# Both seams of a two-layer diffusion block redone, and later landings in the planner that orders it

## The chip, the cores and the metric

The kernel runs on one core of one Trainium2 chip. Its time is the device time of one execution in microseconds. The kernel before takes 2654.45 us, the median of three runs (2653.88 to 2655.54).

## The reference

A backbone of two layers works on 512 latent tokens and 256 context tokens, 1024 wide, all in float32. Cut to what matters here:

```
for l in range(2):
    zx = modulate(rms_norm(x, g_norm1[l]), ...) @ w_in[l]      # and zc from the context tokens
    k, q, v, gates = parts of zx;  kc, vc = parts of zc        # K and V are the first thing formed
    yc = windowed_attention(rope(q), rope(k), v, kc, vc, sink[l])
    ya = bidirectional RG-LRU;  yb = spatial gating MLP
    x = x + ga1 * ((ga*(ya@wb0) + gb*(yb@wb1) + gc*(yc@wb2)) @ w_out[l])
    x = x + ga2 * relu2(modulate(rms_norm(x, g_norm2[l]), ...) @ w_ff1[l]) @ w_ff2[l]
    # the context tokens go the same way in layer 0 and are dropped after layer 1's K, V and scan states
```

There are two kinds of seam in it. An RMS norm needs all of x, so the first matrix product after a norm waits for the residual sum before it: once where the MLP of layer 0 ends and K and V of layer 1 begin, and once in each layer where the output projection ends and the MLP begins.

## The kernel before

Activations lie with channels on the partitions and tokens along the row: 768 columns in layer 0 (512 latent, 256 context), 512 in layer 1. Each product is taken in three parts: a weight block of 128x1024 comes from DRAM as `wr`, ScalarE rounds it to `wh`, VectorE forms the rest `wl` = wr - wh, activations are split in the same way, and TensorE adds wh.h, wh.l and wl.h in PSUM (`fm`, line 866; 24 matmuls a block, 128 output channels and a token range). There are three buffers each of wr, wh and wl (line 49), and 48 slots for activations.

The order of the instructions is not that of the code. All operations are recorded first, and `schedule` (line 337) plans them on the five engines with a cost for each: an operation may be taken up to `WINDOW` = 275 operations ahead of the oldest one not yet done (line 407), if a buffer is free, and the one of the highest priority that is ready in the plan's own time goes first. For a DMA the plan takes bytes/360 ns on one shared line and 1900 ns for the landing (lines 471 and 472), whatever engine issues it. Each engine then works through its list in that order on the chip, and waits where the plan was wrong.

Around the seams the MLP is written as eight chunks (`ff`, line 1401): chunk c of the first product (4 blocks, relu and square) one ahead of chunk c of the second (4 blocks, each giving two output ranges, added to x at once). So that a norm has something to lie beside, some blocks are done by token streams (`streams`, line 811: 0 to 512 and 512 to 768 in layer 0, 0 to 256 and 256 to 512 in layer 1): first stream 1 of these blocks, then the norm of stream 1, then stream 2 of the same blocks, whose weights are loaded and split again. By streams go: the last six of the eight blocks of the output projection (`JOINT` = 2 are done whole, line 525), the first chunk of the MLP, and in layer 0 the last chunk of its second product.

Of layer 1, 44 weight blocks are split already during the MLP of layer 0 and stored in DRAM as pairs (`store`, line 587; `hd` and `ld` in the rows), when VectorE and ScalarE have room. `weights` (line 574) fetches a stored pair into a wh and a wl buffer. The four blocks 112 to 115 are those of K and V of layer 1 (`B_K`), used by `kv_proj` (line 945) right behind the seam, once for the latent and once for the context tokens. `kv_post` (line 951) then forms the constants of the layer, `layer_consts` (line 742: rope tables, sink, the softplus of the LRU, some forty small VectorE instructions, one Exp on ScalarE and three DMAs of GpSimd).

`mod_dve` (line 713) forms one column of the modulation vectors: a wr buffer with rows of w_mod, times the condition, summed (the `junk<-wr,condb` rows). These run beside the merges of the branches.

Of the kernel before, what the change touches and what calls it, by code (L numbers as in the profile page):

```python
# [19 lines left out]
F32R = mybir.dt.float32r  # L20
BF16 = mybir.dt.bfloat16
I32 = mybir.dt.int32
AF = mybir.ActivationFunctionType
# [5 lines left out]
DEPTH = 2  # L29
# [28 lines left out]
LAZY = 200  # L58
DRAINS = 50
FULL, URGENT = 6, 150  # L60
WINDOW = 275
TABLES = {"Sigmoid": (2,), "Sqrt": (3,), "Gelu_apprx_tanh": (11,), "Exp": (0,), "Tanh": (0, 2, 11)}

# [119 lines left out]
class Rec:  # L183
# [153 lines left out]
    def schedule(self):  # L337
# [90 lines left out]
        while events:  # L428
            now = events[0][0]
            while events and events[0][0] <= now + 1e-6:  # L430
                _, _, kind, x = heapq.heappop(events)
                if kind == "rel":
                    used[x.tag] -= 1
                    places[x.tag].append(x)
                    live[x.tag][x.first:x.last + 1] -= 1
                    if x.early:
                        early[x.tag][x.early[0]:x.early[1]] -= 1
            for e in range(5):
                while free[e] <= now + 1e-6:
                    best = pick(e)  # L440
                    if best is None:
                        break
                    _, j, i = best
                    cand[e].pop(j)
                    op = ops[i]
                    for b in op.new:
                        if b.space == "dram":
                            continue
                        used[b.tag] += 1
                        b.early = None  # L450
                        b.prev = places[b.tag].pop(0)
                        if b.prev is None:
                            b.place = fresh[b.tag]
                            fresh[b.tag] += 1
                        else:
                            b.place = b.prev.place
                        if b.first > front:
                            b.early = (front, b.first)
                            early[b.tag][front:b.first] += 1
                    dur = op.dur  # L460
                    if op.both and free[POOL] > now and busy:
                        dur += free[POOL] - now
                    if e == POOL:
                        busy = not op.nbytes
                    if e == ACT and op.table and table not in op.table:
                        dur += 1283
                        table = op.table[0]
                    free[e] = now + dur
                    end = now + dur
                    if op.nbytes:  # L470
                        dma = max(dma, end) + op.nbytes / 360.0
                        end = dma + 1900
                    op.end = end
                    for b in op.psum:
                        b.acc[e] = end
                    order.append((now, i))
                    done[i] = True
                    push(free[e], "go", None)
                    for u in op.users:
                        q = ops[u]  # L480
                        r = end + (LAT if op.nbytes else LATS[e][q.eng])
                        q.ready = max(q.ready, r)
                        q.wait -= 1
                        if q.wait == 0:
                            bisect.insort(cand[q.eng], (q.prio, u))
                            push(q.ready, "go", None)
                    for b in op.bases:
                        b.left -= 1
                        b.end = max(getattr(b, "end", 0.0), end)
                        if b.left == 0 and b.space != "dram":  # L490
                            push(b.end + LAT, "rel", b)
                    while done[front]:
                        front += 1
# [28 lines left out]
AHEAD_C = ('', '0', '1', '2', 'k', '')  # L522
AHEAD_X = ('', '0', '1', 'k')
NEAR = 60
JOINT = (2,)
EARLY = [*range(B_K, B_F2), *range(B_G, B_P), *range(B_AX, B_V)]


# [1 line left out]
class Net:  # L530
# [43 lines left out]
    def weights(self, l, blk):  # L574
        rec = self.rec
        rec.boost, was = self.wboost, rec.boost
        if (l, blk) in self.stored:
            hi = self.wtile("wh", [128, 1024], F32R)
            lo = self.wtile("wl", [128, 1024], F32R)
            for t, d in zip((hi, lo), self.stored[l, blk]):  # L580
                rec.sync.dma_start(t.bitcast(F32), d.bitcast(F32))
        else:
            hi, lo = self.parted(l, blk)
        rec.boost = was
        return hi, lo
# [365 lines left out]
    def kv_post(self, l, ps, pairs):  # L951
        nc = self.nc
        if pairs[0] == 0:
            self.layer_consts(l)
            self.kr, self.VS = [], []
        n = 8 * len(pairs)
        ss = self.tiny(n, "kss")
        h3 = lambda u: u.rearrange("p (a d) -> p a d", d=64)
        for c, i in enumerate(pairs):
            q = self.slot([128, 512])  # L960
            for t in range(2):
                nc.scalar.activation(q[:, t * 256:t * 256 + 256], ps[2 * i + t][:, 0:256], AF.Square)
            nc.vector.tensor_reduce(ss[:, c * 8:c * 8 + 8], h3(q), axis=AX.X, op=OP.add)
        rs = self.head_rs(ss, n, 1.0, "k")
        for c, i in enumerate(pairs):
            u = self.slot([128, 512])
            for t in range(2):
                nc.vector.tensor_mul(h3(u[:, t * 256:t * 256 + 256]), h3(ps[2 * i + t][:, 0:256]),
                                     rs[:, c * 8 + t * 4:c * 8 + t * 4 + 4, None].to_broadcast([128, 4, 64]))
            o = self.slot([128, 512])  # L970
            if i < 2:
                self.rope_rows(u, 2, 2 * i, o)
            else:
                self.gain_rows(u, 2, o)
            self.kr.append(o)
        for t in range(2 * pairs[0], 2 * pairs[-1] + 2):
            v = self.slot([128, 4, 128], F32R)
            s = ps[t][:, 256:512].rearrange("p (g d) -> p g d", d=64)
            nc.scalar.activation(v[:, :, 0:64], s, AF.Copy)
            nc.vector.tensor_sub(v[:, :, 64:128], s, v[:, :, 0:64].bitcast(F32))  # L980
            self.VS.append(v)
# [419 lines left out]
    def ff(self, l, hs, W):  # L1401
        nc = self.nc

        def ff1(c, parts):
            out = [(self.slot([128, W], F32R), self.slot([128, W], F32R)) for _ in range(4)]
            for z in parts:
                for j in range(4):
                    w = self.weights(l, B_F1 + 4 * c + j)
                    if len(parts) == 1:
                        self.ahead()  # L1410
                    ps = self.fm(w, hs, z)
                    for p, a, b in ps:
                        r = self.slot([128, b - a])
                        nc.scalar.activation(r, p, AF.Relu)
                        nc.vector.tensor_mul(r, r, r)
                        self.split(r, out[j][0][:, a:b], out[j][1][:, a:b])
            return out

        def ff2(c, z, parts):
            for j in range(4):  # L1420
                w = self.weights(l, B_F2 + 4 * c + j)
                if c < 7:
                    self.ahead()
                for i in range(2):
                    ps = self.fm(w, z, parts, kk=4, off=i * 128, stride=256)
                    self.residual(l, 40, ps, 2 * j + i)

        z = ff1(0, [[q] for q in self.streams(W)])
        self.aside = False
        for c in range(7):  # L1430
            for _ in range(3):
                self.bg()
            z2 = ff1(c + 1, [self.parts(W)])
            ff2(c, z, self.parts(W))
            z = z2
        if l == DEPTH - 1:
            ff2(7, z, self.parts(W))
            return
        self.mod_bias(l + 1, 0, 16)
        hs = self.pairs(TOK)  # L1440
        G = self.gain(l + 1, 0, TOK)
        ps = [self.p1() for _ in range(6)]
        for q in self.streams(W):
            ff2(7, z, [q])
            self.norm(l + 1, 0, hs, G, *q)
        for toks in (range(4), range(4, 6)):
            self.kv_proj(l + 1, hs, ps, toks)
            self.kv_post(l + 1, ps, (0, 1) if toks[0] == 0 else (2,))
        return hs, ps

    def run(self):
# [149 lines left out]
```

## Time and profile before

| | |
|---|---|
| median of the runs | 2654.45 us |
| the profiled execution | 2655.47 us |
| its span, first to last instruction | 2653.7 us |
| TensorE busy | 2604.5 us (98%) |
| VectorE busy | 1840.1 us (69%) |
| ScalarE busy | 1200.1 us (45%) |
| granted TensorE clock, mean | 0.995 |

The span is what the instructions cover; the profiled execution's own time is 1.8 us more. TensorE is the engine with almost no idle time, so a change shows in the total where it takes a wait of TensorE away, adds one, or changes how long matmuls run. All recorded operations carry the line of the helper that emits them (L508), so rows are told apart by tiles: p is a PSUM tile, s an activation slot, wh and wl the parts of a weight block, t a small tile.

### The profile page before, as it was taken

The numbers are of one execution on the slowest core, as the hardware profiler recorded it, in microseconds if no ns is written. First come the engines' busy times: TensorE is split into PE (matmuls) and PEld (weight loads), VectorE is DVE, ScalarE is ACT, GpSimd is POOL, SyncE is SP. The second block draws the span as 40 slices with busy tenths as digits, with TensorE's granted clock in tenths as the row PEclk, the third lists the DMA queues.
The fourth block names the chain that finished last, engine by engine and source line by source line (L and its number), as shares of the span: only waits on it lengthen the run. The fifth ranks groups of instructions, "written<-read, shape, count | busy, mean of one in ns | idle before, by whom it ended". The sixth has DMA issues, their size and how long they took to land.

```text
span 2653.7 us, 38578 instructions
## 1 busy us (share of the span) xinstructions
PE 2604.5 (98%) x14916; PEld 2246.2 (85%) x14916; DVE 1840.1 (69%) x3504; ACT 1200.1 (45%) x1987; POOL 122.7 (5%) x217
## 2 busy tenths in 40 slices
PE   7999999999999999999999989999999999999999
PEld 4989988888898888888888878888887888888887
DVE  8888776997637748465666678886986567844444
ACT  4566557993122225332333334667993233532322
POOL 1000000011000000100111000000011000000000
PEclk9999999999999999999999999999999999999999
DMA  6122213466425424766778634334577565533332
GB/s 248 45 69 74 61 56 104 122 198 226 154 80 165 162 79 134 230 214 199 246 261 263 207 134 169 105 121 154 159 245 248 165 189 178 158 95 96 95 93 83
DMA packets 129528, 403.54 MB, mean 152 GB/s; under 512 B 15232, under 2 KB 25632, under 8 KB 129344
## 3 DMA queue, kind: packets, MB, share of 16 engines
q1 hardware_dynamic: 99360, 302.11, 36.3%
q0 software_dynamic: 23072, 83.24, 9.4%
q10 hardware_dynamic: 6912, 15.73, 1.6%
q8 instruction: 117, 1.92, 0.3%
q14 instruction: 67, 0.55, 0.1%
HBM read 319.23 MB, written 81.79 MB: 151 GB/s over the span
## 4 chain that ended last, share of the span: by engine, by line
PE 69%; DVE 6%; ACT 3%; issue 1%; DMA 1%; ACTq 0%; DVEq 0%; POOLq 0%
PE p L508 69%; DVE s L508 4%; ACT s L508 3%; DVE wl L508 1%; DMA wr<-wmod 1%; DVE t L508 1%; ACT L508 0%; ACT wh L508 0%; DMA ya<-s 0%; DVE junk L508 0%; ACTq L508 0%; DVEq L508 0%; POOLq L508 0%
## 5 line engine op out<-in xcount | busy, mean ns | idle before, releaser
L508 PE MATMUL p<-s,wh 128*128 128x512 f32 (+1 forms) x6816 | 1670.7, 353 | 8.8 <-DVE s L508 6.1
L508 PEld LDWEIGHTS p<-s,wh 128*128 128x128 f32 x6816 | 1192.0, 189 | 239.7 <-DVE s L508 7.8
L508 PE MATMUL p<-s,wl 128*128 128x512 f32 (+1 forms) x3408 | 1028.5, 351 | 8.8 <-DVE wl L508 8.8
L508 ACT ACTIVATE wh<-wr 128x1024 fp32r<-128x1024 f32 x336 | 354.8, 1059 | 871.7 <-PE p L508 475.0
L508 PEld LDWEIGHTS p<-s,wl 128*128 128x128 f32 x3408 | 570.3, 189 | 58.2 <-DVE wl L508 11.1
L508 DVE TENSOR_TENSOR wl<-wr,wh 128x1024 fp32r<-128x1024 f32 x336 | 409.7, 1222 | 291.8 <-ACT wh L508 249.6
L508 ACT ACTIVATE s<-p 128x512 f32<-128x512 f32 (+6 forms) x598 | 282.0, 511 | 271.1 <-PE p L508 255.2
L508 PE MATMUL p<-wh,s 128*128 128x256 f32 (+1 forms) x1472 | 301.9, 298 | 1.7 <-DVE s L508 1.0
L508 DVE TENSOR_TENSOR s<-s,s 128x512 fp32r<-128x512 f32 (+5 forms) x361 | 258.1, 728 | 53.4 <-ACT s L508 49.0
L508 PE MATMUL p<-s,s 128*128 128x256 f32 (+3 forms) x1568 | 279.9, 319 | 5.9 <-ACT s L508 3.9
L508 ACT ACTIVATE s<-s 128x512 fp32r<-128x512 f32 (+6 forms) x301 | 182.5, 633 | 195.7 <-DVE s L508 179.3
L508 PEld LDWEIGHTS p<-s,s 128*128 128x128 f32 (+1 forms) x1568 | 219.5, 183 | 41.0 <-DVE s L508 7.3
L508 PEld LDWEIGHTS p<-wh,s 128*128 128x128 f32 x1472 | 236.3, 188 | 13.7 <-DVE s L508 2.3
L508 DVE SCALAR_TENSOR_TENSOR s<-p,mod,s 128x512 f32<-128x512 f32 (+1 forms) x222 | 138.7, 646 | 156.2 <-PE p L508 155.5
L508 PE MATMUL p<-wl,s 128*128 128x256 f32 (+1 forms) x736 | 217.9, 296 | 1.0 <-DVE wl L508 1.0
L508 DVE SCALAR_TENSOR_TENSOR junk<-wr,condb 128x1024 bf16<-128x1024 f32 x128 | 156.4, 1222 | 86.7 <-DMA wr<-wmod 85.7
L508 DVE TENSOR_TENSOR s<-p,s 128x512 fp32r<-128x512 f32 (+4 forms) x324 | 182.8, 595 | 37.3 <-ACT s L508 31.5
L508 PEld LDWEIGHTS p<-wl,s 128*128 128x128 f32 x736 | 138.5, 188 | 6.6 <-DVE wl L508 1.6
L508 ACT ACTIVATE s<-s,t,t 128x512 f32<-128x512 f32 (+1 forms) x128 | 109.9, 863 | 50.2 <-DVE t L508 49.8
L508 DVE SCALAR_TENSOR_TENSOR s<-s,s 128x768 f32<-128x768 f32 x128 | 116.7, 949 | 16.2 <-ACT s L508 16.2
L508 PE MATMUL p<-ident,s 128*128 128x128 f32 (+1 forms) x776 | 102.9, 274 | 5.2 <-DVE s L508 3.1
L508 PEld LDWEIGHTS p<-ident,s 128*128 128x128 f32 (+1 forms) x776 | 88.4, 142 | 14.1 <-ACT s L508 3.5
(90 smaller groups left out, 1236.2 us busy)
## 6 DMA issues: line engine op xcount, KB each, us to landing
wr<-w SPq DMA_DIRECT2D x336, 512.0 KB, 3.8
wr<-wmod SPq DMA_DIRECT2D x80, 512.0 KB, 4.2
wl<-ld SPq DMA_DIRECT2D x48, 512.0 KB, 4.8
wh<-hd SPq DMA_DIRECT2D x48, 512.0 KB, 3.7
hd<-wh POOLq DMA_DIRECT2D x44, 512.0 KB, 3.7
ld<-wl POOLq DMA_DIRECT2D x44, 512.0 KB, 5.6
gd<-s ACTq DMA_DIRECT2D x24, 384.0 KB, 2.6
s<-gd POOLq DMA_DIRECT2D x24, 384.0 KB, 5.7
```

Source lines behind the costliest of these rows:

```text
L508: ins = getattr(getattr(self.nc, name), method)(*[r(x) for x in a], **{q: r(x) for q, x in k.items()})
```

## The change

Six things. The planner takes 2600 ns for the landing of a DMA of SyncE or ScalarE and 4800 ns for one of GpSimd, in place of 1900 ns for all. Fetches of the stored K blocks may be planned at most `CLOSE` = 160 operations ahead in place of 275. The constants of layer 1 are formed in the MLP of layer 0, after its fourth round and at a low priority, not behind the seam. Two of the four blocks of chunk 6 of the second product in layer 0 move behind chunk 7 of the first product and are done by streams, together with those of chunk 7. In layer 1 two of the four blocks of chunk 1 of the first product are done by streams, together with those of chunk 0. One block of the output projection is done whole in place of two.

```diff
+LANDS = {SP: 2600, ACT: 2600, POOL: 4800}
@@ schedule
                         dma = max(dma, end) + op.nbytes / 360.0
-                        end = dma + 1900
+                        end = dma + LANDS[e]
@@
+CLOSE = 160
+CONSTS = 4
+SPLIT = 2
+OVER = (0, 1)
+THIRDS = ((0, 512), (512, 768))
-JOINT = (2,)
+JOINT = (1,)
@@ weights
+            rec.far = CLOSE if B_K <= blk < B_Q else None
             for t, d in zip((hi, lo), self.stored[l, blk]):
                 rec.sync.dma_start(t.bitcast(F32), d.bitcast(F32))
+            rec.far = None
@@ kv_post
         if pairs[0] == 0:
-            self.layer_consts(l)
+            if l == 0:
+                self.layer_consts(l)
@@ ff
-        def ff1(c, parts):
-            out = [(self.slot([128, W], F32R), self.slot([128, W], F32R)) for _ in range(4)]
-            for z in parts:
-                for j in range(4):
+        def room():
+            return [(self.slot([128, W], F32R), self.slot([128, W], F32R)) for _ in range(4)]
+        def ff1(c, parts, out, js=range(4)):
+            for j in js:
...
-        z = ff1(0, [[q] for q in self.streams(W)])
+        z, z1 = room(), room() if l == DEPTH - 1 else None
+        for q in self.streams(W):
+            ff1(0, [q], z)
+            if z1:
+                ff1(1, [q], z1, OVER)
         for c in range(7):
...
-            z2 = ff1(c + 1, [self.parts(W)])
-            ff2(c, z, self.parts(W))
+            if c == CONSTS and l < DEPTH - 1:
+                rec = self.rec
+                rec.boost, was = -LAZY, rec.boost
+                self.layer_consts(l + 1)
+                rec.boost = was
+            if c == 0 and z1:
+                z2 = ff1(1, self.parts(W), z1, [j for j in range(4) if j not in OVER])
+            else:
+                z2 = ff1(c + 1, self.parts(W), room())
+            ff2(c, z, self.parts(W), range(4) if c < 6 or l == DEPTH - 1 else range(SPLIT))
...
-        for q in self.streams(W):
+        for q in THIRDS:
+            ff2(6, z6, [q], range(SPLIT, 4))
             ff2(7, z, [q])
             self.norm(l + 1, 0, hs, G, *q)
```

In SyncE's list before the seam between the layers, before the change, the lo part of block 112 and of block 113 stand ahead of the last five raw blocks of the MLP:

```order
L508 DMA wr_14765<-w 128x1024
L508 DMA wl_14789<-ld_112_10941 128x1024
L508 DMA wh_14793<-hd_112_10919 128x1024
L508 DMA wr_14821<-w 128x1024
L508 DMA wl_14877<-ld_113_11019 128x1024
L508 DMA wr_14949<-w 128x1024
L508 DMA wr_14988<-w 128x1024
L508 DMA wr_15028<-w 128x1024
L508 DMA wr_15068<-w 128x1024
L508 DMA wr_15110<-w 128x1024
L508 DMA wh_15225<-hd_113_11000 128x1024
```

At the same place after the change, up to the hi part of block 113:

```order
L509 DMA wr_14919<-w 128x1024
L509 DMA wr_14958<-w 128x1024
L509 DMA wr_14998<-w 128x1024
L509 DMA wr_15038<-w 128x1024
L509 DMA wl_15066<-ld_112_10960 128x1024
L509 DMA wr_15113<-w 128x1024
L509 DMA wl_15206<-ld_113_11038 128x1024
L509 DMA wh_15248<-hd_112_10944 128x1024
L509 DMA wh_15300<-hd_113_11028 128x1024
```

One raw block follows the first fetch of a lo part, where six did, and none follows the second, where five did.

On TensorE, behind the second norm's broadcast (`ones`) in the MLP of layer 1, before the change; the rows ahead of it are the last of stream 1, those behind it the first two blocks of stream 2:

```order
L508 MATMUL p_22805<-s_22679,wh_22710 128x256
L508 MATMUL p_22805<-s_22609,wl_22725 128x256
L508 MATMUL p_22849<-s_22839,ones 128x256
L508 MATMUL p_22885<-s_22528,wh_22749 128x256
L508 MATMUL p_22885<-s_22592,wh_22749 128x256
L508 MATMUL p_22885<-s_22528,wl_22770 128x256
L508 MATMUL p_22890<-s_22528,wh_22809 128x256
```

After the change; p_22895 is the fifth block of stream 1:

```order
L509 MATMUL p_22895<-s_22551,wh_22801 128x256
L509 MATMUL p_22895<-s_22612,wh_22801 128x256
L509 MATMUL p_22895<-s_22551,wl_22815 128x256
L509 MATMUL p_22906<-s_22886,ones 128x256
L509 MATMUL p_22895<-s_22573,wh_22801 128x256
L509 MATMUL p_22895<-s_22635,wh_22801 128x256
L509 MATMUL p_22895<-s_22573,wl_22815 128x256
```

Six of the fifth block's 24 matmuls stand ahead of the broadcast; 18 of it and 24 of the sixth stand between the broadcast and the first of stream 2.

On VectorE, where the merge of the last branch begins in layer 1, before the change; `s<-s,s` of 512 are the lo parts of its eight inputs, junk is a column of the modulation:

```order
L508 TENSOR_TENSOR s_20482<-s_19995,s_20255 128x512
L508 TENSOR_TENSOR s_20489<-s_20026,s_20480 128x512
L508 TENSOR_TENSOR s_20498<-s_20063,s_20487 128x512
L508 SCALAR_TENSOR_TENSOR junk,mod_10721<-wr_20467,condb 128x1024
L508 TENSOR_TENSOR wl_20521<-wr_20462,wh_20493 128x1024
L508 TENSOR_TENSOR s_20537<-s_20086,s_20507 128x512
L508 SCALAR_TENSOR_TENSOR s_20363<-s_20363,p_20472 128x512
L508 TENSOR_TENSOR s_20551<-s_20096,s_20515 128x512
L508 TENSOR_TENSOR s_20556<-s_20113,s_20519 128x512
```

After the change:

```order
L509 TENSOR_TENSOR s_20530<-s_20075,s_20505 128x512
L509 TENSOR_TENSOR wl_20539<-wr_20479,wh_20516 128x1024
L509 TENSOR_TENSOR s_20548<-s_20102,s_20512 128x512
L509 SCALAR_TENSOR_TENSOR s_20385<-s_20385,p_20487 128x512
L509 TENSOR_TENSOR s_20560<-s_20109,s_20532 128x512
L509 TENSOR_TENSOR s_20567<-s_20131,s_20541 128x512
L509 TENSOR_TENSOR s_20572<-s_20207,s_20543 128x512
L509 TENSOR_TENSOR s_20577<-s_20497,s_20565 128x512
L509 SCALAR_TENSOR_TENSOR junk,mod_10735<-wr_20500,condb 128x1024
```

The column of the modulation stands behind the lo parts of all eight inputs, where it stood behind three of them.

## Rows read from the trace of the kernel before

**Rows 1.** The page: the span, and busy time of each engine.

```profile
span 2653.7 us, 38578 instructions
PE 2604.5 (98%) x14916; PEld 2246.2 (85%) x14916; DVE 1840.1 (69%) x3504; ACT 1200.1 (45%) x1987; POOL 122.7 (5%) x217
```

**Rows 2.** Waits of TensorE, whole span: us in total, times, longest.

```profile
PE p L508 <- DVE s L508: 22.5, 17, 6.6
PE p L508 <- DVE wl L508: 9.8, 9, 2.5
PE p L508 <- ACT s L508: 8.3, 10, 1.7
```

**Rows 3.** Waits of TensorE at the seam between the layers, 1515 to 1566 us.

```profile
PE p L508 <- DVE wl L508: 8.8, 7, 2.5
PE p L508 <- DVE s L508: 1.0, 1, 1.0
```

**Rows 4.** Waits of TensorE at layer 1's norm, 2290 to 2306 us.

```profile
PE p L508 <- DVE s L508: 3.4, 2, 2.2
PE p L508 <- ACT s L508: 1.7, 1, 1.7
```

**Rows 5.** Waits of TensorE where layer 1's last merge begins, 2036 to 2046 us.

```profile
PE p L508 <- DVE s L508: 3.3, 1, 3.3
PE p L508 <- ACT s L508: 0.5, 1, 0.5
```

**Rows 6.** Stretches: length, busy us of PE, PEld, DVE, ACT, POOL, clock, DMA.

```profile
1030.00:1515.00 485.00, 485.00 (x2795) 424.92 (x2794) 290.85 (x444) 162.91 (x234) 48.51 (x91) 1.00 0.70 229
1552.30:1555.80 3.50, 3.23 (x13) 2.71 (x13) 2.21 (x8) 0.59 (x2) 0.00 (x0) 0.51 0.00 0
2043.80:2050.70 6.90, 5.22 (x12) 4.05 (x13) 5.86 (x9) 0.14 (x1) 1.08 (x2) 0.51 0.94 338
2299.80:2306.70 6.90, 5.07 (x23) 5.07 (x24) 5.22 (x14) 1.98 (x5) 0.00 (x0) 0.51 0.19 69
```

**Rows 7.** Timeline of SyncE and VectorE at the seam: start, us, what.

```profile
1500.87 0.33 SPq L508 DMA_DIRECT2D wl<-ld  x1
1509.27 0.32 SPq L508 DMA_DIRECT2D wl<-ld  x1
...
1549.04 0.16 DVE L508 TENSOR_SCALAR t<-p 128x4 f32<-128x4 f32 x1 [0.75 <-PE p L508]
...
1551.29 1.22 DVE L508 TENSOR_TENSOR wl<-wr,wh 128x1024 fp32r<-128x1024 f32 x1
```

**Rows 8.** Timeline of TensorE, layer 1: matmuls of 512 and of 256 columns.

```profile
2030.31 0.40 PE L508 MATMUL p<-s,wl 128*128 128x512 f32 x1
...
2040.07 0.40 PE L508 MATMUL p<-s,wl 128*128 128x512 f32 x1
...
2280.12 0.28 PE L508 MATMUL p<-s,wl 128*128 128x256 f32 x1
...
2285.07 0.28 PE L508 MATMUL p<-s,wl 128*128 128x256 f32 x1
...
2296.63 0.70 PE L508 MATMUL p<-s,ones 128*128 128x256 f32 x2 [1.18 <-DVE s L508]
...
2302.01 0.42 PE L508 MATMUL p<-s,wl 128*128 128x256 f32 x1
...
2302.66 0.41 PE L508 MATMUL p<-s,wl 128*128 128x256 f32 x1
```

**Rows 9.** Timeline of VectorE where layer 1's last merge begins.

```profile
2042.45 1.22 DVE L508 SCALAR_TENSOR_TENSOR junk<-wr,condb 128x1024 bf16<-128x1024 f32 x1 [2.82 <-DMA wr<-wmod]
```

**Rows 10.** DMA issues: engine, count, KB each, median us from issue to landing.

```profile
wr<-wmod SPq DMA_DIRECT2D x80, 512.0 KB, 4.2
wl<-ld SPq DMA_DIRECT2D x48, 512.0 KB, 4.8
ld<-wl POOLq DMA_DIRECT2D x44, 512.0 KB, 5.6
```

More of the change, by code (lines that the diff above doesn't have):

```diff
@@ L1402, in ff, with ff2 @@
         nc = self.nc
-        def ff1(c, parts):
-            out = [(self.slot([128, W], F32R), self.slot([128, W], F32R)) for _ in range(4)]
-            for z in parts:
-                for j in range(4):
[L1408 to L1416, printed above, removed]
-            return out
-        def ff2(c, z, parts):
-            for j in range(4):
+        def room():
+            return [(self.slot([128, W], F32R), self.slot([128, W], F32R)) for _ in range(4)]
+        def ff1(c, parts, out, js=range(4)):
+            for j in js:
+                w = self.weights(l, B_F1 + 4 * c + j)
+                if len(parts) == len(self.parts(W)):
+                    self.ahead()
+                ps = self.fm(w, hs, parts)
+                for p, a, b in ps:
+                    r = self.slot([128, b - a])
+                    nc.scalar.activation(r, p, AF.Relu)
+                    nc.vector.tensor_mul(r, r, r)
+                    self.split(r, out[j][0][:, a:b], out[j][1][:, a:b])
+            return out
+        def ff2(c, z, parts, js=range(4)):
+            for j in js:
                 w = self.weights(l, B_F2 + 4 * c + j)
@@ L1432, in ff @@
                 self.bg()
-            z2 = ff1(c + 1, [self.parts(W)])
-            ff2(c, z, self.parts(W))
-            z = z2
+            if c == CONSTS and l < DEPTH - 1:
[8 more added lines that the diff above has]
+            ff2(c, z, self.parts(W), range(4) if c < 6 or l == DEPTH - 1 else range(SPLIT))
+            z, z6 = z2, z
         if l == DEPTH - 1:
@@ L1442, in ff @@
         ps = [self.p1() for _ in range(6)]
-        for q in self.streams(W):
+        for q in THIRDS:
+            ff2(6, z6, [q], range(SPLIT, 4))
             ff2(7, z, [q])
             self.norm(l + 1, 0, hs, G, *q)
-        for toks in (range(4), range(4, 6)):
-            self.kv_proj(l + 1, hs, ps, toks)
-            self.kv_post(l + 1, ps, (0, 1) if toks[0] == 0 else (2,))
+        for a, b in THIRDS:
+            self.kv_proj(l + 1, hs, ps, range(a // 128, b // 128))
+            self.kv_post(l + 1, ps, tuple(range(a // 256, b // 256)))
         return hs, ps
```

## Prediction

> **What bounds the kernel now.** I read the page first: TensorE is busy 2604.5 of 2653.7 us [rows 1], so a gain has to come from what little time it waits, or from matmuls that run at half clock. Next the waits of TensorE alone: 22.5 us for activations from VectorE, 9.8 for lo parts of weight blocks, 8.3 for ScalarE [rows 2]. Then the same view by stretches, to see where these stand. Three short places hold 18.7 of those 40.6 us: the seam between the layers, 8.8 + 1.0 [rows 3]; the norm in layer 1 ahead of its MLP, 3.4 + 1.7 [rows 4]; the start of the last merge in layer 1, 3.3 + 0.5 [rows 5]. The rest, some 22 us, is spread over the start and the attention stages. In the MLP of layer 0, 485 us long, TensorE is busy for the whole of it [rows 6].
>
> Last the granted clock by stretches. At each of the three places it reads 0.51, half rate (1.2 in place of 2.4 GHz), for 3.5 or 6.9 us right behind the wait [rows 6]. What this costs can be read from matmuls of 256 columns: three of them take 0.65 us at half rate (2302.01 to 2302.66) and 0.354 at full rate (2280.12 to 2285.07 holds 14 such triples) [rows 8]. So 45% of the busy time in a slow stretch is loss: 0.45 x 3.23 = 1.5 us, 0.45 x 5.22 = 2.3 us, 0.45 x 5.07 = 2.3 us for the three places in the order of rows 6.
>
> **The change part by part.**
>
> *Seam between the layers.* Waits 9.8 and clock 1.5, 11.3 us in all. Seven of the eight waits are for a lo part. The reason is in the timeline: two fetches of stored lo parts go out at 1500.87 and 1509.27 [rows 7] and occupy two of the three wl buffers until K is formed, some 55 us later. The five raw blocks behind them share one buffer, so VectorE may subtract only when TensorE has finished with the last lo part; the subtraction takes 1.22 us [rows 7], the hi parts of the next block cover part of it, and TensorE waits some 0.9 us each time. In the new list of SyncE one raw block follows the first of these fetches and none the second, so at most the last two blocks are left in that position. I count the five short waits and the shorter long ones as gone. What is late next: VectorE works in order, and in the trace the longest wait, 2.5 us, comes from the chain of the norm's inverse root that starts at 1549.04 ahead of the subtraction at 1551.29 [rows 7]. Norm and subtraction stay neighbours in the new seam, so I keep 2.5 us for one such wait. Gain 8.8 us; bounds 4 (two blocks of the last kind, the K product still waiting 1.0, the clock still falling) and 11.3.
>
> *Two blocks more by streams there.* Stream 2 now has six blocks behind norm 1 in place of four. A block is 24 matmuls of 256 columns, 8 triples of 0.354 us, 2.8 us; the norm of stream 1 has 5.7 us more to lie beside. This makes the 2.5 us above a wait inside the stretch rather than a start of K that waits; no gain of its own is counted.
>
> *Norm of layer 1.* Waits 5.1, clock 2.3, 7.4 us in all. Before, the broadcast stands behind the fourth block of stream 1, and nothing but stream 2 behind it, which needs the norm. From the broadcast at 2296.63 to the stream running without a break at 2302.01 are 5.4 us [rows 8]. In the new list 30 matmuls (0.118 each, 3.5 us) lie ahead of the broadcast that did not, more than the 1.2 us that it waited, and 42 (5.0 us) between it and stream 2. That leaves 0.4 us. VectorE also gets two subtractions more in this stretch (2 x 1.22), which can lie ahead of the norm's own work: up to 2.4 us worse. I take 0.8 left and no fall of the clock: gain 6.6, bounds 4 and 7.4.
>
> *Last merge of layer 1.* Waits 3.8, clock 2.3, 6.1 us in all. VectorE stood 2.82 us before a column of the modulation whose rows had not landed (junk, [rows 9]), and behind it in the list stood the lo parts of five of the merge's inputs. The plan had reckoned 1900 ns for a landing beside the bytes; such a DMA takes 4.2 us at the median [rows 10]. With 2600 ns the column is put behind all eight lo parts, as the new list of VectorE shows. Late next would be the lo parts for ScalarE, a fraction of a microsecond (0.5 in [rows 5]). Gain 5.6; bounds 0 (the wait comes back before another column) and 6.1.
>
> *Landings elsewhere.* The new figures reorder all five engines in every stage, so each of the small waits (some 22 us in all, the start's among them) may move. I count 0, with 4 us either way: a wait of the size of one at the merge may go or come.
>
> *What is added.* Six more raw blocks are loaded, rounded and subtracted (two for chunk 0 and 1 of layer 1, two in the seam, one in each output projection). They cost ScalarE and VectorE some 1 us each a block, beside a full TensorE; without that cover each would be a wait like those at the seam, 0.9 us, 5.4 in all. On TensorE three blocks of layer 1 are split from 512 into 2 x 256 columns: 24 triples a half as long, twice as many. A triple of 512 takes 0.697 us (2030.31 to 2040.07 holds 14), two of 256 take 0.708 [rows 8]; 24 x 0.011 = 0.2 us. The constants of layer 1 (some forty small instructions, one Exp with a table of its own) move from a stretch where they stood ahead of the waits into one where TensorE does not wait and VectorE is busy 290.85 of 485 us [rows 6]: 0, and up to 3 us if the Exp and its table hold up a rounding. I take 0.5.
>
> **Sum.** -8.8 - 6.6 - 5.6 + 0.2 + 0.5 = -20.3 us. Against the profiled execution, 2655.5, that gives 2635.2. The median of the runs is 1.0 lower than that execution, so I forecast 2634 us, 0.77% less.
>
> **The rivals.**
>
> *The landing assumption moves the wait of the merge and does not remove it.* Then the merge's 5.6 is lost: 2640 us. For it: columns of the modulation come all along the merges, and half of their fetches land later than 4.2 us [rows 10], more than the plan's new figure covers. Against: the new list has no merge input behind the column.
>
> *The K blocks now come late.* In the new list the hi part of block 112 goes out after the last raw block, and the K product begins soon behind. For it: a stored lo part takes 4.8 us to land [rows 10], and if it is issued only when a buffer falls free at the end, TensorE waits about that long once, and runs at half clock behind it: 4.8 + 1.5 = 6.3, so 2640 us. Later blocks would be covered, since one serves 24 matmuls of 512 columns for the latent tokens, 5.6 us. Against: a whole raw block (2.8 us) and the rest of the norm lie between. The Trainium skill ("DMA: Bandwidth & Descriptors", rules for kernel authors) says to issue a DMA early and wait on it late; by that rule the fetch in advance was right, and moving it back gives this rival's time. The trace shows the price of early issue that the rule leaves out, two of three buffers held [rows 3, 7], and I weigh that more.
>
> *Slower: the planner holds buffers longer in the MLP of layer 0.* 44 blocks are split and stored there; a buffer is freed by the landing of its store, and the plan now takes 4800 ns where it took 1900. If this leaves the weights of the MLP with one free wl buffer as at the seam, each stored block costs 0.9 us: 44 x 0.9 = 40 us, and with -20 the time is 2674 us. It outweighs the gain from 23 blocks on. For it: the stores are real buffer holders (5.6 us to land, [rows 10]). Against: the landing is the same as before, the plan is nearer to it now, and the stretch had no wait at all with a plan that was too hopeful.
>
> *Hidden or given back.* The three waits go, but others of the same size come with the new order: 2654 us. The lists speak against it at all three places.
>
> **Chances.** Forecast 0.60, with 2626 to 2642 as its own range; wait of the merge stays 0.17; K late 0.13; slower 0.05; given back 0.05. Lower end of the range: all 24.8 us of the three places and 4 elsewhere, 2626; I set 2625. Upper end: the lower bounds of the first two places (4 + 4), and the merge gaining nothing, 2647. A difference under 0.2% (5.3 us) cannot be told from no change here. Faster 0.90, within it 0.05, slower 0.05.
>
> **What would show it.** Between 1500 and 1560 us the waits of TensorE for lo parts should be one or two, no more than 4 us together. Behind layer 1's norm broadcast the matmuls should go on and the wait be under 1.5 us, with no slow stretch of the clock there nor at the last merge. The MLP of layer 0 should show hardly any wait. Wrong would be: K blocks as releaser of a wait by DMA at the seam; a wait of several us before a junk column with the merge behind it; waits for lo or hi parts strewn over 1030 to 1500 us.

## The result and the profile after

The changed kernel takes 2623.85 us (median; 2623.65 to 2625.99, 4 runs), the kernel before, run beside it, 2654.16 (2650.16 to 2655.54, 4 runs). The ratio is 0.989, with a 95% interval of 0.9873 to 0.9907: 30 us less, where I had forecast 20. The direction and the gains at the three places came out much as described. The time lies 1.15 us below my range, mostly because the new landing figures also took waits away in stretches for which I had counted 0.

The page of the kernel after, span and busy time of the engines (the rows that answer to [rows 1]):

```profile
span 2623.4 us, 38749 instructions
PE 2598.2 (99%) x14988; PEld 2247.3 (86%) x14988; DVE 1851.0 (71%) x3515; ACT 1205.8 (46%) x1998; POOL 122.6 (5%) x217
```

TensorE has 72 matmuls more and is busy 6.3 us less: up to its last matmul, the clock stood at half for 23.8 us before and for 13.6 after, and 45% of the difference, 4.6 us, is by my estimate loss that is gone. The larger part is waits. The same view as [rows 2], kernel after (us in total, times, longest):

```profile
PE p L509 <- DVE s L509: 8.8, 12, 4.8
PE p L509 <- ACT s L509: 4.6, 7, 1.8
PE p L509 <- DMA s<-wmod_k: 3.5, 1, 3.5
PE p L509 <- DVE wl L509: 1.8, 2, 1.5
PE p L509 <- ACT wh L509: 1.1, 1, 1.1
PE p L509 <- DVE G L509: 0.7, 1, 0.7
```

All waits of TensorE together fell from 44.2 to 20.4 us. Waits for activations from VectorE went from 22.5 to 8.8, waits for lo parts from 9.8 to 1.8. Some 3 us of this fall stand in the first 60 us and bought nothing there: in the profiled execution of the kernel after, the clock was at half for 10.2 us of the start, where it had been for 3.4. At the three places, the answers to [rows 3] and [rows 4] follow. First the seam between the layers, 1490 to 1590 us:

```profile
PE p L509 <- DVE wl L509: 1.5, 1, 1.5
PE p L509 <- DVE s L509: 0.3, 1, 0.3
```

Then layer 1's norm, 2200 to 2330 us:

```profile
PE p L509 <- DVE s L509: 0.7, 2, 0.4
```

For [rows 5], the last merge of layer 1, there is nothing to show: from 2000 to 2200 us TensorE waits for no one. The stretches of the kernel after that hold the three places, and two more (length; busy us of PE, PEld, DVE, ACT, POOL; granted clock; DMA share; GB/s):

```profile
1540.00:1560.00 20.00, 18.25 (x117) 15.85 (x116) 19.15 (x36) 9.33 (x17) 0.00 (x0) 1.00 0.39 134
2030.00:2050.00 20.00, 20.00 (x88) 16.18 (x87) 12.69 (x17) 3.30 (x4) 1.07 (x2) 1.00 0.75 235
2270.00:2290.00 20.00, 19.33 (x159) 18.87 (x158) 19.48 (x41) 13.52 (x28) 0.00 (x0) 1.00 0.49 155
450.70:454.10 3.40, 3.40 (x13) 2.91 (x12) 3.37 (x5) 3.40 (x8) 0.00 (x0) 0.50 0.00 0
1030.00:1490.00 460.00, 458.56 (x2650) 401.97 (x2650) 280.70 (x428) 155.83 (x226) 47.34 (x89) 1.00 0.72 230
```

The clock is 1.00 at all three places, where it read 0.51 in [rows 6]. A new slow stretch stands at 450.7 us, in layer 0's LRU, and the MLP of layer 0, which had no idle time at all in [rows 6], now has 1.4 us.

To see where the 30 us came from I cut both profiles at the same points of TensorE's work (matmul columns streamed, weighted by their mean spacing; other weights shift the figure for the norm of layer 1, where blocks were split, by some half a microsecond) and compared the stretches; the spans, 2653.7 and 2623.4, differ by 30.3 us. Stretches by the times of before:

| stretch, us | after less before |
|---|---|
| 0 to 60, start | +1.2 |
| 60 to 600, layer 0's attention and LRU | -4.1 |
| 600 to 1030 | -0.75 |
| 1030 to 1490, MLP of layer 0 | +1.35 |
| 1490 to 1590, seam | -11.2 |
| 1590 to 2000 | -0.9 |
| 2000 to 2070, last merge of layer 1 | -6.7 |
| 2070 to 2180, behind that merge | -2.9 |
| 2180 to 2330, norm of layer 1 | -6.9 |
| 2330 to the end | +0.6 |

The three places gave 24.8 us. Some 7 us came from stretches for which I had counted nothing.

### The profile page after: what moved, and what is told of

It is laid out like the page before. It is cut to its first block, busy times and chain, and to the rows that moved or that the text cites. A ratio compares the mean times of both kernels' runs of the same rounds, so it can differ in the third digit from the quotient of the medians.

```text
span 2623.4 us, 38749 instructions
## 1 busy us (share of the span) xinstructions
PE 2598.2 (99%) x14988; PEld 2247.3 (86%) x14988; DVE 1851.0 (71%) x3515; ACT 1205.8 (46%) x1998; POOL 122.6 (5%) x217
## 3 DMA queue, kind: packets, MB, share of 16 engines
q8 instruction: 117, 1.92, 0.3%
## 5 line engine op out<-in xcount | busy, mean ns | idle before, releaser
L509 ACT ACTIVATE wh<-wr 128x1024 fp32r<-128x1024 f32 x342 | 361.6, 1059 | 855.2 <-PE p L509 648.9
L509 DVE TENSOR_TENSOR wl<-wr,wh 128x1024 fp32r<-128x1024 f32 x342 | 417.7, 1222 | 239.6 <-ACT wh L509 232.5
L509 DVE SCALAR_TENSOR_TENSOR junk<-wr,condb 128x1024 bf16<-128x1024 f32 x128 | 156.3, 1221 | 52.9 <-DMA wr<-wmod 51.8
```

The costliest lines, as they stand in the source:

```text
L509: ins = getattr(getattr(self.nc, name), method)(*[r(x) for x in a], **{q: r(x) for q, x in k.items()})
```

## The experiments

Ten kernels, each timed in turns against the kernel before, whose median lay between 2652.4 and 2654.2 us in all groups. "Equal work" below means the comparison of the table above. It compares single profiled executions, and the start alone, which no edit aims at, differs by up to 3.7 us from one to another; so it shows where time went, and the medians show how much. Where a run is compared with the kernel after, the two medians come from different groups, and the kernel before moved by up to 1.8 us between groups.

### e1 and e2: the new landing figures alone, and everything but them

The main question: were the 7 us the planner's new figures, and what was the merge worth? e1 is the kernel before with

```diff
+LANDS = {SP: 2600, ACT: 2600, POOL: 4800}
-                        end = dma + 1900
+                        end = dma + LANDS[e]
```

and e2 the kernel after with

```diff
-LANDS = {SP: 2600, ACT: 2600, POOL: 4800}
+LANDS = {SP: 1900, ACT: 1900, POOL: 1900}
```

> The kernel before with the new landings alone (2600 ns, 4800 ns for GpSimd). Theory of the prediction: only the wait at the last merge of layer 1 goes, 5.6 us with its slow clock, all else 0: 2648.5 us. Rival: the landings also take away small waits in layer 0's attention and LRU, and around 2080 to 2150 us, together 6 to 8 us more, so 2641 to 2643 us; both seams keep their waits (9.8 and 5.1 us) in either case.

> The changed kernel with 1900 ns for every landing as before; the rest of the change stays. Prediction's theory: the wait at the merge is back and nothing else, 2623.9 + 5.6 = 2629.5 us. Rival (landings carry the gain outside the three places): 2623.9 + 12 = 2636 us, the waits at 2080 to 2150 us and in the LRU of layer 0 back too. The wait at 1337 us in the MLP of layer 0 (1.15 us) should go if longer store landings make it, and stay if the constants make it.

Measured: e1 2641.23 us (ratio 0.9955, 0.994 to 0.9969), 11.7 less than the kernel before beside it. e2 2636.87 us (0.9939, 0.9924 to 0.9954), 13.0 more than the kernel after. So this one part of the change, which I had put at 5.6 + 0, is worth about 12. By equal work e1 gains 6.7 at the merge, 4.6 between 60 and 600 us and 3.2 behind the merge, and loses 1.2 in the MLP. That is the pattern of the stretches I had not counted. In e2 the wait at the merge is back (waits of TensorE, 2000 to 2070 us; then, as a second answer of the view, 2070 to 2200):

```profile
PE p L509 <- DVE s L509: 3.1, 2, 2.9
...
PE p L509 <- DVE s L509: 1.3, 2, 1.1
PE p L509 <- DVE wl L509: 0.5, 1, 0.5
```

The mechanism is seen on VectorE, which works through its list in order. Its waits on landings, whole span, kernel before:

```profile
DVE junk L508 <- DMA wr<-wmod: 85.7, 52, 4.3
...
DVE wl L508 <- DMA ld<-wl: 32.1, 17, 3.7
```

Kernel after:

```profile
DVE junk L509 <- DMA wr<-wmod: 51.8, 36, 3.6
DVE wl L509 <- DMA ld<-wl: 4.7, 3, 2.0
```

ScalarE, which rounds the raw blocks in order, shows the same. Its waits on their landings before:

```profile
ACT wh L508 <- DMA wr<-w: 191.4, 55, 18.2
```

and after:

```profile
ACT wh L509 <- DMA wr<-w: 108.5, 34, 9.0
```

The runs tie this to the figures: with the new ones alone (e1) VectorE waits 42.2 us for such columns and ScalarE 106.4 for raw blocks; with all of the change but them (e2) it is 88.6 and 195.1.

The transfers did not become much quicker. Issue to landing, kernel after (engine, count, KB, median us), against 4.2, 4.8 and 5.6 in [rows 10]:

```profile
wr<-wmod SPq DMA_DIRECT2D x80, 512.0 KB, 3.9
wl<-ld SPq DMA_DIRECT2D x48, 512.0 KB, 4.7
...
ld<-wl POOLq DMA_DIRECT2D x44, 512.0 KB, 5.5
```

What changed is what stands in the list behind an instruction that waits for a landing. In the kernel after, VectorE still stands 1.92 us before a column of the modulation at the last merge (timeline of VectorE: start, us, what, in brackets the wait and its releaser):

```profile
2034.66 1.23 DVE L509 SCALAR_TENSOR_TENSOR junk<-wr,condb 128x1024 bf16<-128x1024 f32 x1 [1.92 <-DMA wr<-wmod]
2035.81 0.08 DVE L509 DVE_READ_ACCUMULATOR junk<-wr,condb 128x1 f32 x1
2035.88 0.69 DVE L509 SCALAR_TENSOR_TENSOR s<-s,p 128x512 f32<-128x512 f32 x1
```

TensorE does not wait there. The stall of VectorE is 0.9 us shorter than in [rows 9], and what the merge needs no longer stands behind it.

### e10 and e11: the two queues apart

Which of the two figures does it? Both are the kernel before with the lines of e1, and in e10 `LANDS = {SP: 2600, ACT: 2600, POOL: 1900}`, in e11 `LANDS = {SP: 1900, ACT: 1900, POOL: 4800}`.

> The kernel before with 2600 ns for landings of SyncE and ScalarE alone, GpSimd's left at 1900 ns. Theory: the fetches that VectorE and ScalarE stand waiting for in order (columns of the modulation, raw blocks) are SyncE's, so this part carries all that the two figures together gave (2641.2 us): 2641 to 2643 us, the waits at the merge and at 2080 to 2150 us gone. Rival: GpSimd's part carries the gain in layer 0 (its loads feed the merges, its stores end the buffers' use): 2645 to 2647 us here.

> The kernel before with 4800 ns for landings of GpSimd alone, SyncE's and ScalarE's left at 1900 ns. Theory: little or nothing, 2651 to 2656 us, and the wait at the last merge of layer 1 (3.8 us) is still there in some form. Rival: the part of the gain in layer 0, 4 to 6 us, comes from here: 2647 to 2649 us.

Measured: e10 2645.51 us (0.9973, 0.9963 to 0.9984), 7.7 less than before; e11 2651.67 (0.9996, 0.9986 to 1.0005), not to be told from before. The figure for SyncE and ScalarE, which covers the weight loads, carries most, and the merge with it (6.5 us by equal work). With it alone VectorE waits 48.5 us for columns of the modulation and ScalarE 118.9 for raw blocks, nearly as little as in e1. The figure for GpSimd alone brings nothing, but added to the other it brings some 4 more. Neither theory had that. e11 is no idle edit, though. Its waits of TensorE from 60 to 990 us:

```profile
PE p L509 <- DVE s L509: 8.8, 4, 5.5
PE p L509 <- ACT s L509: 4.4, 5, 1.7
PE p L509 <- DVE G L509: 0.7, 1, 0.7
```

and from 1490 to 1600 us:

```profile
PE p L509 <- DVE wl L509: 3.3, 2, 1.7
PE p L509 <- DVE s L509: 0.9, 2, 0.6
```

At the seam it won 8.6 us by equal work: its plan happened to fetch K later, the second lo part only behind the last raw block. Between 600 and 990 us, at the end of layer 0's LRU, a new wait of 5.5 us and the slow clock beside it cost 7.9. It ends at 614.5 us, and the stall of the merge stands ahead of it on VectorE:

```profile
601.92 1.23 DVE L509 SCALAR_TENSOR_TENSOR junk<-wr,condb 128x1024 bf16<-128x1024 f32 x1 [5.29 <-DMA wr<-wmod]
```

In all, its VectorE still waits 85.6 us for columns of the modulation and its ScalarE 170.9 for raw blocks. So a figure in the planner moves waits of several us about in both directions, and two such moves can cancel.

### e3 and e8: the later fetch at the seam, taken away and alone

e3 is the kernel after with

```diff
-CLOSE = 160
+CLOSE = 275
```

which is the reach that all other fetches have. e8 is the kernel before with

```diff
+CLOSE = 160
+            rec.far = CLOSE if B_K <= blk < B_Q else None
+            rec.far = None
```

> The changed kernel with the stored K blocks planned up to 275 operations ahead as before. Theory (held wl buffers make the seam's waits): the short waits of 0.9 us return, and as the stretch by streams now has twelve blocks in place of eight, there are seven to nine of them with a long one: 8 to 10 us more, 2632 to 2634 us. Rival (the two blocks more by streams cover the seam by themselves): under 3 us more, below 2627 us.

> The kernel before with the later fetch of the stored K blocks alone. Theory: about half of the seam's waits go (the short ones), the long ones stay since the norm has only four blocks beside it: 5 to 6 us less, 2648 to 2649 us. Rival (the fetch then comes late): a wait of TensorE for a DMA of 4 to 5 us at the start of the K product, no gain, 2654 us.

Measured: e3 2635.34 us (0.9931, 0.9916 to 0.9946), 11.5 more than after; e8 2645.01 (0.9964, 0.995 to 0.9979), about 8 less than before. By equal work it lies between 1490 and 1590 us: 11.8 and 8.4. Apart from the start, no other stretch moves by more than 0.7 us in e3 or 1.8 us in e8. Waits of TensorE there, in e3:

```profile
PE p L509 <- DVE wl L509: 8.3, 7, 2.5
PE p L509 <- DVE s L509: 1.0, 1, 1.0
```

These are the waits of [rows 3] again (8.8, seven times, longest 2.5) with everything else of the change in place. In the kernel after SyncE fetches the lo parts that K needs only here (timeline of SyncE):

```profile
1532.05 0.33 SPq L509 DMA_DIRECT2D wl<-ld  x1
1536.17 0.33 SPq L509 DMA_DIRECT2D wr<-w  x1
1542.87 0.33 SPq L509 DMA_DIRECT2D wl<-ld  x1
1545.72 4.88 SPq L509 DMA_DIRECT2D wh<-hd  x2
```

Against 1500.87 and 1509.27 in [rows 7] the two buffers are held over 30 us less, and one raw block lies between. No DMA releases a wait of TensorE in this stretch: nothing of K comes late. That the buffers were the cause is seen in what VectorE's subtractions wait for. If TensorE holds the last free wl buffer, they wait for TensorE. Waits of VectorE, 1515 to 1566 us, in e3:

```profile
DVE wl L509 <- PE p L509: 4.0, 4, 2.1
```

and in the kernel after:

```profile
DVE wl L509 <- PE p L509: 0.3, 1, 0.3
```

### e4: no blocks of chunk 1 by streams in layer 1

```diff
-OVER = (0, 1)
+OVER = ()
```

> The changed kernel with chunk 1 of layer 1's MLP whole again (no block of it by streams). Theory: the two blocks by streams are what covers the norm of layer 1, so its waits of 5.1 us and the slow clock of about 2 us return, 2623.9 + 6.7 = 2630 to 2631 us, and nothing else moves. Rival (the landings had already let VectorE finish the norm earlier): under 3 us more, below 2627 us.

Measured: 2631.39 us (0.9917, 0.9903 to 0.993), 7.5 more than after, some 7 of it between 2270 and 2330 us by equal work. The waits of TensorE, 2200 to 2330 us, are much like those of [rows 4]:

```profile
PE p L509 <- DVE s L509: 4.3, 2, 3.3
PE p L509 <- ACT s L509: 1.1, 1, 1.1
```

and the clock falls for 6.8 us behind them. My 6.6 us for this place stands.

### e5: no blocks of the last chunk but one by streams at the seam

```diff
-SPLIT = 2
+SPLIT = 4
```

> The changed kernel with chunk 6 of the second product of layer 0 whole again, so that four blocks lie behind norm 1 at the seam in place of six. Theory: the later fetch does most at the seam and the two blocks a smaller part; the norm then ends in a wait of 2 to 3.5 us, 2626 to 2628 us. Rival (the blocks do as much as the fetch): 5 us or more, above 2629 us.

Measured: 2628.51 us (0.9905, 0.9891 to 0.9918), 4.7 more than after. The intervals overlap and one of its four runs, 2624.68, lies among those of the kernel after, so the medians alone leave the size open. By equal work 3.1 us lie in the seam; 1.3 more lie behind the merge of layer 1, which has no block of this edit. Waits of TensorE, 1490 to 1590 us:

```profile
PE p L509 <- DVE wl L509: 3.6, 2, 1.9
```

and behind the second, 1.9 us at 1551.9, the clock reads 0.50 for 3.4 us. So the two blocks more, to which I gave "no gain of its own", keep about 2 us of waiting and, in this execution, a fall of the clock away.

### e6: the constants of layer 1 behind the seam again

```diff
-            if l == 0:
-                self.layer_consts(l)
+            self.layer_consts(l)
-            if c == CONSTS and l < DEPTH - 1:
+            if False:
```

> The changed kernel with the constants of layer 1 formed behind the seam as before. Theory (they stood beside a full TensorE, so moving them gave nothing, and cost a wait of 1.4 us at 1337 us): 1 to 2 us less, 2622 to 2623 us. Rival (they held up VectorE at the seam): 3 us or more slower, 2627 us. If the wait in the MLP of layer 0 stays, the longer landings of the stores make it and not the constants: then 2624 us.

Measured: 2624.34 us (0.9891, 0.9877 to 0.9905), level with after. The waits that are new in layer 0's MLP stay (waits of TensorE, 1035 to 1490 us):

```profile
PE p L509 <- ACT wh L509: 0.8, 1, 0.8
PE p L509 <- DVE wl L509: 0.3, 1, 0.3
```

So the moved constants are not needed for them. e1 and e10, with the constants in their old place and the new figure for SyncE, have them too (0.7 and 0.3; 0.8 and 1.7). e11, without that figure, has none: the one wait of 0.5 in this window is the norm's, which stands at 1026.7 us before. But the figures are not needed either: e2, with the old ones and the constants moved, has one wait of 1.1, and its MLP is 1.4 us longer by equal work, as much as in the kernel after. Either part of the change goes with a loss of that size, and together they give no more. Which of them acts in the kernel after is not shown. On the time, where the constants stand makes no difference that can be measured here.

### e9: three settings together

The kernel after with the constants as in e6, three blocks by streams in place of two at the seam and at layer 1's norm, and all blocks of the output projections by streams (`JOINT` counts those taken over the whole width first):

```diff
-SPLIT = 2
-OVER = (0, 1)
-JOINT = (1,)
+SPLIT = 1
+OVER = (0, 1, 2)
+JOINT = (0,)
```

> A version made from what the runs show: the changed kernel with the constants behind the seam again, no block of the output projection whole, three of the four blocks of chunk 6 (layer 0) and of chunk 1 (layer 1) by streams in place of two. Theory: the last waits at both norms (0.7 and 1.8 us) and at the output projection (0.4 us) and the one of 1.4 us in the MLP shrink, 3 to 4 us in all: 2620 us. Rival: each block by streams loads and splits its weights twice, and VectorE, in order, is late with a norm for it: 2624 us or more.

Measured: 2621.91 us (0.9882, 0.9868 to 0.9895), 1.9 below after by medians. It is the fastest run of all, but the intervals overlap, so it is not shown to beat the kernel after. Of the waits at the seam one is left, 1490 to 1590 us:

```profile
PE p L509 <- DVE s L509: 0.2, 1, 0.2
```

and none at layer 1's norm. These two places have nothing more to give.

## Why the prediction was right in kind and short by 10 us

- **What bounds the kernel, and the three places.** Right. Of 24.8 us that I read there (11.3 + 7.4 + 6.1, waits and slow clock), 24.8 went by equal work. I had booked 21.0 of it.
- **Seam, -8.8.** The mechanism is right (e3, e8); the term was too small by 2.4: it measured -11.2. I kept 2.5 us for a wait for VectorE, whose in-order work puts the norm ahead of a subtraction. The wait is there, for that reason, at 1.5 us, and the clock did not fall behind it, so the half clock went too. Timeline of VectorE there, kernel after:

```profile
1542.83 3.37 DVE L509 SCALAR_TENSOR_TENSOR s<-s,G,p 128x512 f32<-128x512 f32 x5
1546.13 1.22 DVE L509 TENSOR_TENSOR wl<-wr,wh 128x1024 fp32r<-128x1024 f32 x1
```

  Five steps of the norm, 3.37 us, go ahead of the subtraction that TensorE needs. The step that I put at nothing has its part in its being shorter:
- **Two blocks more by streams, 0.** Too small: without them the seam is 3.1 us longer by equal work (e5).
- **Norm of layer 1, -6.6.** It measured -6.9, and e4 takes some 7 away. One reading was off: I counted 30 matmuls more ahead of the broadcast. That many more do stand between the two broadcasts, but between the second norm's own sums and its broadcast there are only 15 more (48 where 33 were), 1.8 us, still more than the 1.2 that it waited. I had kept 0.8 us of wait; 0.7 is left. Timeline of TensorE, kernel after, the broadcast and the start of stream 2:

```profile
2272.48 0.70 PE L509 MATMUL p<-s,ones 128*128 128x256 f32 x2 [0.28 <-DVE s L509]
...
2278.62 0.39 PE L509 MATMUL p<-s,wh 128*128 128x256 f32 x1 [0.39 <-DVE s L509]
```

- **Last merge, -5.6.** It measured -6.7; no wait is left where I kept a fraction. e1 gives the same 6.7 from the landing figures alone.
- **Landings elsewhere, "I count 0".** This is the step that failed. I priced the landing figures at the merge's 5.6 us; they measured 11.7 alone (e1) and 13.0 taken away (e2). Outside the three places and the MLP about 7 us went: 4.1 from 60 to 600 us, 2.9 behind the merge, the rest in small amounts of both signs. e1 gains the first two with nothing else changed (4.6 and 3.2). I had seen that each small wait could move and took both directions as equally likely, with 4 us either way. But the figures moved towards what the trace shows for a landing, and the same in-order stall that I had traced at the merge, a junk column before a buffer that something else needs, stood in other places: in all VectorE waits 85.7 us for such columns before and 51.8 after, ScalarE 191.4 and 108.5 for raw blocks. One of the latter cost TensorE time. Timeline of ScalarE, kernel before:

```profile
376.15 1.06 ACT L508 ACTIVATE wh<-wr 128x1024 fp32r<-128x1024 f32 x1 [6.16 <-DMA wr<-w]
```

  It stands 6.16 us before a raw block not yet landed; TensorE waits for what follows (2.4 us), and its clock is at half for 3.4 us from 385.0 on. This place gave 3.3 us by equal work, some 1.5 of it the slow clock, and the new wait at 450 us took 3.6 back; the rest of the 4.1 are waits between 408 and 560 us. Not all are traced to such a stall: at 537.0, where 1.3 us of waiting went, ScalarE is busy for the 6 us ahead and waits for no landing. One question to the trace, which waits of VectorE and ScalarE are on landings, would have given this term a sign.
- **Split columns and constants, +0.2 and +0.5.** The columns were not measured by themselves. The constants cost nothing that can be measured (e6). The MLP did lose 1.35 us where I had booked 0.5; with the landing figures alone (e1) it loses 1.2, without them (e2) 1.4, so my reason is neither shown nor refuted.
- **The block of the output projection, no term.** At layer 0's norm, 990 to 1030 us, 1.2 us went. e2 has this gain and e1 has not, so it is not the landing figures; this block is the only other part of the change that touches the place, but it was not run alone.
- **Rivals.** *The wait of the merge stays*: no, it went whole. *K comes late*: no wait of TensorE at the seam ends with a DMA. The early fetch is 11.5 us slower here (e3), since it holds two of three buffers. The rule of the Trainium skill ("DMA: Bandwidth & Descriptors", rules for kernel authors), to issue a DMA early and wait on it late, would have made e3 the better kernel; here the measurement goes the other way. *The planner holds buffers in the MLP of layer 0*: 1.4 us of new wait there, not 40: one or two waits and not one for each stored block. As e2 has a wait of that size with the old figures, even the direction is not shown. *Given back*: new waits did come, but the one in the LRU of layer 0 (1.8 and its slow clock 1.5) and the two in the MLP take back under 5 us, not 20.
- **The range.** Its lower end was the whole of the three places and 4 us elsewhere. Both were reached and the second passed.

What stays open: why the two landing figures together bring some 2.5 us more than the sum of each alone (11.7 against 7.7 + 1.5), beyond that the orders differ. The intervals reach 2.5 to 2.8 us to either side for e10 and e11 and nearly 4 for e1, so this may be chance. By equal work e1 is ahead of e10 by 2.0 us from 60 to 600, 1.4 from 600 to 1030 and 1.8 in the MLP.

## What to carry to other kernels

Where a planner orders in-order engines by assumed landing times, set these from the trace first: an assumption that is too short puts an instruction that waits for a landing ahead of work that is needed now, and the loss can turn up far from the wait that is largest. Here this held for the loads; the figure for GpSimd, moved towards its trace by itself, brought nothing. To size such an edit, sum the waits on landings over all in-order engines, not those of TensorE alone. And a prefetch is paid for in buffers: count how many a waiting block takes from the stream beside it, and for how long.

## What the runs showed of the chip

The length of a wait does not tell what it costs. One wait in layer 0's LRU stands in most of the kernels at the same place, ahead of the same six matmuls. In the kernel after TensorE's granted clock fell to half (1.2 in place of 2.4 GHz) behind it; in e10 it did so behind a shorter one, and in e1 it stayed at full rate behind a longer one. Timelines of TensorE, in this order:

```profile
450.22 1.91 PE L509 MATMUL p<-s,s 128*128 128x512 f32 x6 [1.78 <-ACT s L509]
...
447.88 1.32 PE L509 MATMUL p<-s,s 128*128 128x512 f32 x6 [1.64 <-ACT s L509]
...
448.98 1.32 PE L509 MATMUL p<-s,s 128*128 128x512 f32 x6 [2.15 <-ACT s L509]
```

Likewise the wait of 2.36 us at 383.5 us, with half clock behind it before, is there in e2 with the same 2.36 and the clock stays at full rate. At the seam the clock stayed at full rate behind waits of up to 1.5 us in the kernel after and 1.7 in e8, and fell behind one of 1.9 in e5.

The slow stretch behind the wait of 1.78, 3.4 us at 0.50 in the table of stretches above, costs by my estimate 0.45 x 3.40 = 1.5 us, so that this wait costs 3.3 in all. At the norm and the merge, half clock lasted 6.8 us before, and by the same estimate its end brought 2.3 us each. Shortening a wait a little, from 2.5 to 1.5 us as at the seam, can thus come with more than twice what it shortens. But since waits of one length went either way, a difference of 1.5 us between two profiled executions may be no more than a fall of the clock that one of them had.
